# DeltaNet stage with a fixed TensorE order, block-wise operands one job ahead, weight splits on VectorE and DeltaNet's branch as the last jobs

## The chip, the cores and the metric

The kernel runs on one core of one Trainium2 chip. The metric is device time in microseconds: before the change the median of 3 runs is 1790.77 us (1789.58 to 1791.43).

## The reference, cut to what matters

One layer: a modulated norm, three token mixers fed by one input projection, gates, one output projection, then a gated feed-forward part. The sequence has 512 tokens of width 1024 and a context of 256 tokens that only feeds states. All matrices are float32.

```
proj = h @ w_in
s5   = s5_readout(scan(proj[s5]))            # ends in y * sigmoid(y @ s5_w_glu)
dn   = rms(deltanet(q, k, v, beta, g)) * silu(z)   # 8 heads of 128, both directions
cv   = silu(layernorm(dwconv31(a * sigmoid(gate))))
merged = g0 * (s5 @ w_br_s5) + g1 * (dn @ w_br_dn) + g2 * (cv @ w_br_cv)
x = x + mod * (merged @ w_out)
x = x + mod * convffn(rms(x))
```

DeltaNet works in chunks: each head needs, for each chunk and direction, a triangular inverse and a chain over chunks in which a 128x128 state is carried from one to the next.

## The kernel before, in words

A float32 product of full accuracy is made of three float32r matmuls: each operand is split into a high part (ScalarE rounds it) and a low part (the rest, by VectorE or GpSimd). `weights` (L188) loads 128 output columns of a matrix for all 8 blocks of 128 inputs (512 KB, three buffers), and `split` (L178) makes `whi` and `wlo` from it (two buffers each). Which engine makes `wlo` goes by the letters of `split_plan`; in the DeltaNet stage it is "G", so GpSimd makes them.

The stages are: prologue; S5 with the input projections; the convolution's taps; the DeltaNet stage; the output projection (`mix_out`); the feed-forward part. In the S5 stage TensorE's order is kept as written (`tc.manual_schedule`); in the DeltaNet stage the tile scheduler orders all engines by a simulated timeline. Each engine and SyncE, which issues nearly all loads and stores, works its instructions off in the order it is given.

The DeltaNet stage mixes two kinds of work. `dn` (L1516) runs turns. Every 9 turns a new head starts (`dn_head`, L1302), and in a turn each head that is live does one step, up to its next `yield`. A step is a few TensorE operations (float32, 128 columns, two records each) and what VectorE, ScalarE and GpSimd make of them. A head has 47 steps: decays and k-k products; a 15-step elimination on GpSimd (`dn_tmp`, `dn_dd`); doubling of the inverse for s = 16 and 32; a last doubling; 6 chunks of 3 steps each, where `dn_R`, `dn_vt`, `dn_vn`, `dn_S` are made on VectorE and ScalarE; and `dn_out`. So about 5 heads are live at a time. Between the heads' steps `dn` draws from `fill` until the turn has its planned time (3.8 us, in the kernel's own cost units), and from `side` (S5's gelu, the convolution's norm, then the sums for the second modulation, `ada2_sums`) at 2.8 units a turn.

`fill` is `jobs` (L759): 56 jobs, each 128 output columns of a product with 512 tokens, that is 8 steps of 3 matmuls into one PSUM bank. They are 8 for z, 24 for the gates (both on the normed input `hx`), 8 for S5's GLU, 8 for S5's branch and 8 for the convolution's branch. The last three groups have operands of their own: `once` allots a whole operand (`operand`, [128, 8, 512], high and low) and `split_pieces` loads and splits its 8 blocks; at least two blocks are made before the group's first matmul. A job's weights are loaded while the job before it runs; its result is finished (`fin`) after the first step of the next.

When `dn` and the jobs are over, `dn_load` (L1579) loads and splits the eight heads' results, `merged` is loaded as the sum of the two stored branches, and `branch` (L842) makes the 8 jobs of DeltaNet's branch, with the second modulation's sums (`ada2`, one matmul pair with a matrix of ones each) between them.

PSUM: jobs use banks a and e in turn, the heads' preparation and inverse share the two banks of c, the chunk steps use d and b.

Of the kernel before, what the change touches and what calls it, by code (L numbers as in the profile page):

```python
# [8 lines left out]
F32 = mybir.dt.float32  # L9
F32R = mybir.dt.float32r  # L10
# [6 lines left out]
P = 128  # L17
# [33 lines left out]
class Slab:  # L51
# [5 lines left out]
    def tile(self, shape, dtype, **kw):  # L57
# [7 lines left out]
        return t.rearrange("p (a b) -> p a b", a=shape[1]) if len(shape) == 3 else t  # L65

# [13 lines left out]
class Kern:  # L80
# [307 lines left out]
    def modulate_tokens(self, pool):  # L388
# [3 lines left out]
        self.hx = (hp.tile([P, KT, SEQ], F32R, name="hxh"), hp.tile([P, KT, SEQ], F32R, name="hxl"))  # L392
# [366 lines left out]
    def jobs(self, jobs):  # L759

        T = self.nc.tensor
        load = lambda j: self.weights(self.A[j[0]][0], 0, KT, j[1], P)
        jobs = iter(jobs)
        j, done = next(jobs), None
        nxt = load(j)
        while j:
            _, _, xs, fin = j
            (wh, wl), (ps, j) = nxt, (None, next(jobs, None))  # L770
            prep = iter(())
# [9 lines left out]
            ps = self.psum()  # L781
            for k in range(KT):
# [14 lines left out]
    def z_jobs(self, pool):  # L797
# [3 lines left out]
        def fin(h):  # L801
            def f(pz):
                z = pool.tile([P, SEQ], F32, name="do_z", tag="gt", bufs=3)
# [7 lines left out]
    def gate_jobs(self, pool):  # L811
# [3 lines left out]
        def fin(i):  # L815
            def f(pg):
                t = pool.tile([P, SEQ], F32, name="gt", tag="gt", bufs=3)
# [6 lines left out]
    def branch_jobs(self, gi, wname, xs, pool, out, perm=False):  # L824
# [3 lines left out]
        def fin(m):  # L828
            def f(pb):
                sg = pool.tile([P, SEQ], F32, name="br_sg", tag="gt", bufs=3)  # L830
# [11 lines left out]
    def branch(self, gi, wname, xs, pool, tag, bufs, perm=False):  # L842

        nc = self.nc
        for m in range(KT):
            sg = pool.tile([P, SEQ], F32, name="br_sg", tag=tag, bufs=bufs)
            nc.sync.dma_start(sg, self.gt_d[gi * KT + m])
            pb = self.psum()
            self.mm3(pb, self.weights(self.A[wname][0], 0, KT, m * P, P), xs)
            sv, pv = sg, pb  # L850
            if perm:
                sv = sg.rearrange("p (n t) -> p n t", t=8)
                pv = pb.rearrange("p (t n) -> p n t", t=8)
            nc.vector.scalar_tensor_tensor(sv, sv, 1.0, pv, op0=OP.add, op1=OP.mult)
            yield m, sg


    def operand(self, pool, bufs=2):
# [1018 lines left out]
```

## Time and profile before

| | |
|---|---|
| median of 3 runs | 1790.77 us |
| the profiled execution's own time | 1797.43 us |
| its span, first to last instruction | 1795.6 us |
| mean granted TensorE clock | 0.954 |
| TensorE matmuls busy | 1634.2 us |
| VectorE, ScalarE, GpSimd busy | 1143.3, 706.8, 815.2 us |
| data moved | 268.71 MB |

In the profile PE is TensorE's matmuls, PEld its weight loads, DVE VectorE, ACT ScalarE, POOL GpSimd, SP SyncE. Matmul records overlap: one runs on while the next has started, so their sum is longer than the time they need.

### The profile page before, as it was taken

How to read it: one execution, taken by the hardware profiler on the slowest of the kernel's cores; microseconds unless marked ns; L12 is line 12 of the kernel's file. 1: busy time of each engine (PE TensorE's matmuls, PEld its weight loads, DVE VectorE, ACT ScalarE, POOL GpSimd, SP SyncE). 2: the span in 40 equal slices, each digit the busy share in tenths (PEclk: the TensorE clock that was granted, in tenths of full speed). 3: DMA queues.
4: the chain of work that ended last, by engine and by line, in shares of the span. 5: the costliest groups of instructions: out<-in, count | busy, mean ns of one | idle time of the engine just before them, and what ended most of it. 6: DMA issues, size and time to landing. Idle time of an engine off the chain costs nothing.

```text
span 1795.6 us, 25808 instructions
## 1 busy us (share of the span) xinstructions
PE 1634.2 (91%) x9435; PEld 1324.1 (74%) x9435; DVE 1143.3 (64%) x1958; ACT 706.8 (39%) x1422; POOL 815.2 (45%) x978
## 2 busy tenths in 40 slices
PE   7888898989989988988899989998688899999997
PEld 2677787878878436767788878887466688888886
DVE  6775876678788153466664575544355699999324
ACT  4555344434454224333345544433213233443222
POOL 0647867787784336775365554232133011111020
PEclk9899998999999999998999999999899899999999
DMA  8334323343335887878864544745774133333332
GB/s 299 83 84 120 108 73 97 104 115 105 93 92 157 205 231 222 255 222 261 259 197 141 175 138 132 221 146 176 279 241 142 59 94 99 100 94 100 97 95 73
DMA packets 328689, 268.71 MB, mean 150 GB/s; under 512 B 63333, under 2 KB 264818, under 8 KB 328562
## 3 DMA queue, kind: packets, MB, share of 16 engines
q1 hardware_dynamic: 328130, 266.52, 50.0%
q8 instruction: 74, 1.21, 0.3%
q10 hardware_dynamic: 432, 0.54, 0.1%
q14 instruction: 53, 0.43, 0.1%
HBM read 208.62 MB, written 58.39 MB: 149 GB/s over the span
## 4 chain that ended last, share of the span: by engine, by line
PE 58%; DVE 17%; DMA 12%; issue 5%; ACT 5%; POOL 3%; SPq 1%; DVEq 0%; ACTq 0%; POOLq 0%
PE ps_mm L206 9%; PE ps_mm L207 9%; PE ps_mm L208 8%; PE ps_pr L1318 4%; DMA adw<-in_ada_w_dram 3%; PE ps_mm L783 3%; PE ps_mm L788 3%; PE ps_mm L787 3%; PE ps_acc L1600 3%; PE ps_acc L1601 3%; PE ps_acc L1599 3%; PE ps_inv L1318 2%; DVE wlo L185 2%; DVE ad_acc L321 2%; DVE s5G L664 2%
## 5 line engine op out<-in xcount | busy, mean ns | idle before, releaser
L181 ACT ACTIVATE whi<-wraw 128x1024 fp32r<-128x1024 f32 (+1 forms) x187 | 196.6, 1054 | 379.1 <-PE ps_mm L207 195.6
L185 DVE TENSOR_TENSOR wlo<-wraw,whi 128x1024 fp32r<-128x1024 f32 (+1 forms) x131 | 179.7, 1374 | 173.6 <-ACT whi L181 173.0
L185 POOL TENSOR_TENSOR wlo<-wraw,whi 128x1024 fp32r<-128x1024 f32 x56 | 134.7, 2407 | 166.5 <-ACT whi L181 160.0
L206 PE MATMUL ps_mm<-hxh,whi 128*128 128x512 f32 (+1 forms) x392 | 162.6, 415 | 1.9 <-ACT hxh L403 1.9
L207 PE MATMUL ps_mm<-hxl,whi 128*128 128x512 f32 (+1 forms) x392 | 158.3, 404 | 0.7 <-POOL hxl L404 0.7
L208 PE MATMUL ps_mm<-hxh,wlo 128*128 128x512 f32 (+1 forms) x392 | 157.4, 402 | 0.5 <-DVE wlo L185 0.5
L1698 DVE SCALAR_TENSOR_TENSOR f_acc<-fpad,vec,f_acc 128x512 f32<-128x512 f32 x176 | 152.5, 867 | 3.2
L185 POOL TENSOR_TENSOR hidl<-f_acc,hidh 128x512 fp32r<-128x512 f32 x22 | 36.8, 1672 | 243.0 <-ACT hidh L181 243.0
L206 PE MATMUL ps_mm<-h2h,whi 128*128 128x512 f32 x352 | 137.9, 393 | 0.7 <-ACT h2h L1663 0.7
L207 PE MATMUL ps_mm<-h2l,whi 128*128 128x512 f32 x352 | 137.7, 392 | 0.0
L208 PE MATMUL ps_mm<-h2h,wlo 128*128 128x512 f32 x352 | 137.5, 391 | 0.0
L788 PE MATMUL ps_mm<-hxh,wlo 128*128 128x512 f32 x256 | 105.7, 413 | 8.6 <-POOL wlo L185 8.6
L783 PE MATMUL ps_mm<-hxh,whi 128*128 128x512 f32 x256 | 107.1, 418 | 0.0
L787 PE MATMUL ps_mm<-hxl,whi 128*128 128x512 f32 x256 | 105.3, 411 | 0.0
L206 PEld LDWEIGHTS ps_mm<-hxh,whi 128*128 128x128 f32 (+1 forms) x392 | 76.8, 196 | 17.7 <-ACT hxh L403 2.1
L208 PEld LDWEIGHTS ps_mm<-hxh,wlo 128*128 128x128 f32 (+1 forms) x392 | 75.9, 194 | 18.1 <-DVE wlo L185 0.9
L207 PEld LDWEIGHTS ps_mm<-hxl,whi 128*128 128x128 f32 (+1 forms) x392 | 76.2, 194 | 16.4 <-POOL hxl L404 1.2
L783 PE MATMUL ps_mm<-xh,whi 128*128 128x512 f32 x192 | 78.0, 415 | 5.3 <-DVE rs_t L114 5.3
L787 PE MATMUL ps_mm<-xl,whi 128*128 128x512 f32 x192 | 78.7, 410 | 1.5 <-DVE xl L185 1.5
L788 PE MATMUL ps_mm<-xh,wlo 128*128 128x512 f32 x192 | 78.0, 408 | 0.0
L206 PEld LDWEIGHTS ps_mm<-h2h,whi 128*128 128x128 f32 x352 | 66.6, 190 | 14.8 <-ACT h2h L1663 1.1
L207 PEld LDWEIGHTS ps_mm<-h2l,whi 128*128 128x128 f32 x352 | 66.6, 189 | 13.9
(504 smaller groups left out, 4330.7 us busy)
## 6 DMA issues: line engine op xcount, KB each, us to landing
wraw<-in_w_in_dram SPq DMA_DIRECT2D x80, 512.0 KB
wraw<-in_ffn_w_up_dram SPq DMA_DIRECT2D x44, 512.0 KB
adw<-in_ada_w_dram SPq DMA_DIRECT2D x32, 512.0 KB
wraw<-in_ffn_w_down_dram SPq DMA_DIRECT2D x22, 512.0 KB
cv_y<-cvi SPq DMA_DIRECT2D x32, 270.0 KB
adaw<-in_ada_w_dram SPq DMA_DIRECT2D x16, 512.0 KB
h_d<-dn_Hw SPq DMA_DIRECT2D x16, 384.0 KB
dn_Hb<-h_d SPq DMA_DIRECT2D x8, 768.0 KB
```

What stands on the lines that cost most here:

```text
L181: nc.scalar.activation(hi, x, AF.Copy, scale=scale)
L185: (nc.vector if lo_eng == "V" else nc.gpsimd).tensor_tensor(lo, x, hi, op=OP.subtract)
L206: T.matmul(ps, wh[:, k], xh[:, k], start=first and k == 0, stop=False)
L207: T.matmul(ps, wh[:, k], xl[:, k], start=False, stop=False)
L208: T.matmul(ps, wl[:, k], xh[:, k], start=False, stop=last and k == n - 1)
L783: i = T.matmul(ps, wh[:, k], xh[:, k], start=k == 0, stop=False)
L787: T.matmul(ps, wh[:, k], xl[:, k], start=False, stop=False)
L788: T.matmul(ps, wl[:, k], xh[:, k], start=False, stop=k == KT - 1)
L1318: self.dn_mm = T_.matmul(*a, **kw)
L1599: nc.tensor.matmul(ps[i], xh, wh[:, e], start=k == 0, stop=False)
L1600: nc.tensor.matmul(ps[i], xl, wh[:, e], start=False, stop=False)
L1698: V.scalar_tensor_tensor(acc, pad[:, i:i + R, j:j + W], w(t), acc, op0=OP.mult, op1=OP.add)
```

## The change

1. Operands become lists of 8 tiles of [128, 512] (`Parts`, `block`), one tag and one buffer a block, all in the pool that holds `hx`. `made` builds blocks one at a time; `jobs` has blocks 0 to 6 of the next group's operand made during steps 1 to 7 of the last job before it and the eighth in the group's first job. `ready` holds a block back until its input is there.
2. The group order is z, gates, GLU, convolution's branch, S5's branch, DeltaNet's branch. The last is now 8 more jobs (`merge_jobs`), whose blocks are made as heads end; `dn_load` and `branch` are gone. What `dn` does not draw runs after it.
3. TensorE's order in the stage is the written one (`tc.manual_schedule`), during `dn` and after it.
4. `split_plan` stays "V": `wlo` is made on VectorE.
5. A step that yields a negative number gets so much of `fill` at once and goes on: 0.7 ahead of the k-k products (twice), 1.3 between the halves of the transposes of the inverse. The chunk steps issue all their TensorE operations ahead of what reads them, both directions together; q @ S moves to the chunk's first step.
6. A turn is planned at 3.5 instead of 3.8; small tiles (`gt`) have 5 buffers instead of 3, `dn_at` 6 instead of 4; `conv_norm` yields 9 and 6 more units at its end instead of 2.

The diff, cut to its core:

```diff
+class Parts(list):
+    def __getitem__(self, at):
+        return list.__getitem__(self, at[1])[(at[0], *at[2:])]
...
     def jobs(self, jobs):
-            if callable(xs):
-                if done:
-                    done()
-                    done = None
-                prep, xs = xs()
-                for _ in range(2):
-                    yield next(prep)
-            if xs:
-                xh, xl = xs
+            own = None
+            if callable(xs):
+                own, xs = pend
+            if xs:
+                self.cur = xh, xl = xs
+            (wh, wl), j = nxt, next(jobs, None)
+            ahead = None
+            if j and callable(j[2]):
+                pend = j[2]()
+                ahead, new = pend[0], pend[1][0]
             ps = self.psum()
             for k in range(KT):
+                if len(xh) <= k and done:
+                    done()
+                    done = None
+                while len(xh) <= k:
+                    yield next(own)
                 i = T.matmul(ps, wh[:, k], xh[:, k], start=k == 0, stop=False)
...
-                yield max(0.65, next(prep, 0))
+                c = 0
+                if ahead and k and len(new) < KT - 1:
+                    c = next(ahead)
+                elif own:
+                    c = next(own, 0)
+                yield max(0.65, c)
...
+    def merge_jobs(self, gi, wname, xs, pool, then):
+        def fin(m):
+            def f(pb):
+                sg = pool.tile([P, SEQ], F32, name="br_sg", tag="gt", bufs=5)
+                nc.sync.dma_start(sg, self.gt_d[gi * KT + m])
+                t = pool.tile([P, SEQ], F32, name="mg_t", tag="mg_t", bufs=2)
+                a = self.merged[:, m]
+                nc.sync.dma_start(a, self.m_d[0][m])
+                nc.sync.dma_start(t, self.m_d[1][m])
+                nc.gpsimd.tensor_tensor(a, a, t, op=OP.add)
+                nc.vector.scalar_tensor_tensor(sg, sg, 1.0, pb, op0=OP.add, op1=OP.mult)
+                nc.gpsimd.tensor_tensor(a, a, sg, op=OP.add)
+                next(then, None)
+            return f
...
+    def operand(self, pool, n=KT):
+        x = (Parts(), Parts())
+        for _ in range(n):
+            self.block(x, pool)
+        return x
+    def block(self, x, pool):
+        for t, c in zip(x, "hl"):
+            t.append(pool.tile([P, SEQ], F32R, name="x" + c, tag=f"x{c}{len(t)}", bufs=1))
...
+    def made(self, src, pool, scale=1.0, ready=lambda k: True):
+        def f():
+            x = self.operand(None, 0)
+            def pieces():
+                for k in range(KT):
+                    while not ready(k):
+                        yield 0.1
+                    self.block(x, self.hp)
+                    t = pool.tile([P, SEQ], F32, name="ld", tag="gt", bufs=5)
+                    nc.sync.dma_start(t, src[k])
+                    self.split(x[0][:, k], x[1][:, k], t, scale=scale)
+                    yield 0.7
+            return pieces(), x
+        return f
...
     def dn(self, pool, period, turn_time, fill, side, side_rate):
+                while c is not None and c < 0:
+                    more = -c
+                    while more > 0:
+                        c = next(fill, None)
+                        if c is None:
+                            break
+                        more -= c
+                        t += c
+                    c = next(x[0])
...
-                k.split_plan = "G"
...
+                    yield from k.glu_jobs(cur, k.made(k.y2_d, cur))
+                    yield from k.branch_jobs(2, "w_br_cv", k.made(k.cvc, cur, ready=side_done), cur, k.m_d[1])
+                    yield from k.branch_jobs(0, "w_br_s5", k.made(k.s_d, cur, 0.25), cur, k.m_d[0], perm=True)
+                    yield from k.merge_jobs(1, "w_br_dn", k.made([k.dn_d[i * P:(i + 1) * P] for i in range(HEADS)], cur,
+                                                                 ready=lambda i: i < k.heads_done), cur, others())
                 main = k.jobs(work())
-                k.dn(pool, 9, 3.8, main, itertools.chain(side, sums), 2.8)
+                with tc.manual_schedule(engines={nc.tensor.engine}):
+                    k.dn(pool, 9, 3.5, main, itertools.chain(side, sums), 2.8)
                 k.anchors = []
-                for _ in itertools.chain(main, sums):
+                for _ in sums:
                     pass
-            k.h_stack.close()
-            k.psum_plan(mm="abccddde")
             k.split_plan = "V"
...
-                xs = k.dn_load(pool)
...
+                rest = k.ada2(pool)
+                k.psum_plan(mm="abccddde")
+                with tc.manual_schedule(engines={nc.tensor.engine}):
+                    for _ in main:
+                        pass
+            k.h_stack.close()
```

## Rows read from the trace of the kernel before

**Rows 1.** The page, part 1: busy time of TensorE's matmuls, share of the span, instructions.

```profile
PE 1634.2 (91%) x9435; PEld 1324.1 (74%) x9435; DVE 1143.3 (64%) x1958; ACT 706.8 (39%) x1422; POOL 815.2 (45%) x978
```

**Rows 2.** Stretches: length, busy (instructions) of PE, PEld, DVE, ACT, POOL; clock, DMA share, GB/s.

```profile
120.00:560.00 440.00, 401.20 (x2920) 353.28 (x2919) 335.17 (x460) 201.84 (x433) 344.18 (x423) 0.95 0.36 101
676.00:790.00 114.00, 100.93 (x453) 81.22 (x452) 51.52 (x65) 42.99 (x74) 84.73 (x95) 0.97 0.77 231
790.00:916.00 126.00, 110.72 (x662) 93.39 (x662) 83.47 (x123) 46.23 (x104) 69.39 (x98) 0.93 0.85 257
916.00:1044.00 128.00, 120.27 (x807) 106.83 (x807) 68.30 (x164) 65.83 (x172) 71.41 (x111) 0.93 0.56 162
1044.00:1152.00 108.00, 102.33 (x689) 90.06 (x688) 70.92 (x141) 52.15 (x134) 49.75 (x81) 0.97 0.53 154
1152.00:1278.00 126.00, 114.67 (x642) 96.96 (x639) 53.97 (x143) 42.95 (x102) 38.27 (x19) 0.97 0.55 168
1278.00:1354.00 76.00, 58.87 (x212) 42.11 (x212) 34.10 (x38) 13.31 (x16) 22.54 (x16) 0.87 0.81 277
```

**Rows 3.** TensorE's groups by shape, 676 to 1354 us: busy, mean ns, idle before.

```profile
L788 PE MATMUL ps_mm<-hxh,wlo 128*128 128x512 f32 x247 | 102.1, 414 | 8.6 <-POOL wlo L185 8.6
...
L783 PE MATMUL ps_mm<-xh,whi 128*128 128x512 f32 x192 | 78.0, 415 | 5.3 <-DVE rs_t L114 5.3
L1318 PE MATMUL ps_pr<-dn_S,dn_Ha 128*128 128x128 f32 x288 | 54.9, 283 | 4.3 <-DVE dn_o L1509 4.1 <-DVE dn_S L1497 0.2
...
L206 PE MATMUL ps_mm<-xh,whi 128*128 128x512 f32 x64 | 28.0, 448 | 13.6 <-ACT xh L181 13.2 <-ACT whi L181 0.4
...
L1318 PE MATMUL ps_inv<-dn_TT,dn_xm 64*64 64x64 f32 x192 | 14.9, 227 | 3.6 <-ACT dn_xm L1447 3.6
...
L337 PE MATMUL ps_mm<-ad_acc,ones 128*128 128x512 f32 x16 | 8.5, 614 | 2.0 <-DMA ad_acc<-a_d 2.0
...
L1574 PE MATMUL ps_prep<-ident,dn_o 128*128 128x128 f32 x32 | 5.5, 293 | 5.3 <-POOL dn_o L1567 5.3
```

**Rows 4.** TensorE's timeline: start, length of the merged records, their count.

```profile
1002.59 0.39 PE L787 MATMUL ps_mm<-hxl,whi 128*128 128x512 f32 x1
1002.82 0.39 PE L788 MATMUL ps_mm<-hxh,wlo 128*128 128x512 f32 x1
...
1008.81 0.83 PE L1318 MATMUL ps_pr<-dn_R,dn_TT 128*128 128x128 f32 x6
1009.48 0.83 PE L1318 MATMUL ps_inv<-dn_T,dn_nt 128*128 128x128 f32 x6
...
1290.68 0.63 PE L208 MATMUL ps_mm<-xh,wlo 128*128 128x512 f32 x1
1291.11 0.63 PE L206 MATMUL ps_mm<-xh,whi 128*128 128x512 f32 x1
```

**Rows 5.** TensorE's longest waits, 676 to 1354 us: total, times, longest.

```profile
PE ps_mm L206 <- ACT xh L181: 13.2, 3, 9.4
PE ps_prep L1318 <- DVE dn_T L1417: 12.8, 4, 4.3
PE ps_mm L788 <- POOL wlo L185: 8.6, 6, 2.6
PE ps_mm L783 <- DVE rs_t L114: 5.3, 1, 5.3
PE ps_prep L1574 <- POOL dn_o L1567: 5.3, 1, 5.3
```

**Rows 6.** Groups of weight splits: GpSimd in 676 to 1354, VectorE in 120 to 560 us.

```profile
L185 POOL TENSOR_TENSOR wlo<-wraw,whi 128x1024 fp32r<-128x1024 f32 x54 | 129.9, 2407 | 153.3 <-ACT whi L181 146.9 <-ACT dn_S L1499 6.1 <-PE ps_inv L1318 0.3
...
L185 DVE TENSOR_TENSOR wlo<-wraw,whi 128x1024 fp32r<-128x1024 f32 x39 | 58.8, 1507 | 48.6 <-ACT whi L181 48.5
```

**Rows 7.** Durations of single lines' instructions: count, min/median/max in ns, first to last start.

```profile
L1362 DVE TENSOR_TENSOR kkc<-dn_dm,kkc x8: 412/1336/8157, 686.6 to 1058.5; 128x256 f32<-128x256 f32 x8
...
L1383 POOL TENSOR_TENSOR dn_dd<-dn_dd,dn_tmp x120: 209/315/861, 711.0 to 1119.1; 112x15 f32<-112x15 f32 x16, 112x28 f32<-112x28 f32 x16, 112x39 f32<-112x39 f32 x16, 112x48 f32<-112x48 f32 x16
```

More of the change, by code (lines that the diff above doesn't have):

```diff
@@ L765, in jobs @@
         jobs = iter(jobs)
-        j, done = next(jobs), None
+        j, done, pend = next(jobs), None, None
         nxt = load(j)
@@ L1481, in dn_head @@
                     nc.scalar.activation(vt[d], pr[d][:, P:2 * P], AF.Copy, scale=sc(self.et, d))
-            cost = 0.44
-            for d in range(2):
-                c, x = cs[d], xs[d]
-                if x >= 0:
-                    vn[d] = pool.tile([P, P], F32, name="dn_vn", tag="dn_vn", bufs=4)
-                    nc.scalar.activation(vn[d], pr[d][:, P:2 * P], AF.Copy, scale=self.beta[:, c, 8 * d + h:8 * d + h + 1])
-                    mm(pr[d][:, 3 * P:], kq[:, x, 1], S[d], start=True, stop=True)
-                    cost += 0.22
-            yield cost
-            cost = 0.0
+            for d in seq:
+                x = xs[d]
+                vn[d] = pool.tile([P, P], F32, name="dn_vn", tag="dn_vn", bufs=4)
+                nc.scalar.activation(vn[d], pr[d][:, P:2 * P], AF.Copy,
+                                     scale=self.beta[:, cs[d], 8 * d + h:8 * d + h + 1])
+                if x in seen:
+                    V.scalar_tensor_tensor(o[:, x], pr[d][:, 3 * P:], sc(self.eg, d), o[:, x], op0=OP.mult, op1=OP.add)
+                else:
+                    nc.scalar.activation(o[:, x], pr[d][:, 3 * P:], AF.Copy, scale=sc(self.eg, d))
+                seen.add(x)
+            yield 0.44
             if more:
-                for d in range(2):
+                for d in both:
                     mm(pr[d][:, 2 * P:3 * P], ktok[:, cs[d]], vt[d], start=True, stop=True)
+            for d in seq:
+                mm(pr[d][:, :P], At[d][:, xs[d]], vn[d], start=True, stop=True)
+            if more:
+                for d in both:
                     Sn[d] = pool.tile([P, P], F32, name="dn_S", tag="dn_S", bufs=7)
@@ L1499, in dn_head @@
                         nc.scalar.activation(Sn[d], pr[d][:, 2 * P:3 * P], AF.Copy)
-                    cost += 0.22
-            for d in range(2):
-                x = xs[d]
-                if x >= 0:
-                    mm(pr[d][:, :P], At[d][:, x], vn[d], start=True, stop=True)
-                    if x in seen:
-                        V.scalar_tensor_tensor(o[:, x], pr[d][:, 3 * P:], sc(self.eg, d), o[:, x], op0=OP.mult, op1=OP.add)
-                    else:
-                        nc.scalar.activation(o[:, x], pr[d][:, 3 * P:], AF.Copy, scale=sc(self.eg, d))
-                    late.append((lambda a, b: lambda: V.tensor_tensor(a, a, b, op=OP.add))(o[:, x], pr[d][:, :P]))
-                    seen.add(x)
-                    cost += 0.22
+            for d in seq:
+                late.append((lambda a, b: lambda: V.tensor_tensor(a, a, b, op=OP.add))(o[:, xs[d]], pr[d][:, :P]))
+            cost = 0.22 * ((2 if more else 0) + len(seq))
             S = Sn
@@ L1576, in dn_out @@
         nc.sync.dma_start(self.dn_d[h * P:(h + 1) * P], ot)
+        self.heads_done = h + 1
         yield 0.5
-    def dn_load(self, pool):
-        nc = self.nc
-        dh, dl = self.operand(pool, 1)
-        for h in range(HEADS):
-            t = pool.tile([P, SEQ], F32, name="dn_l", tag="dn_l", bufs=3)
-            nc.sync.dma_start(t, self.dn_d[h * P:(h + 1) * P])
-            self.split(dh[:, h], dl[:, h], t)
-        return dh, dl
     def tok_mm(self, xs, nk, w, fin, pool, tail):
@@ L1801, in open_act, with others, side_done @@
+                def others():
+                    yield from rest
+                def side_done(k_):
                     for _ in side:
                         pass
[L1803 removed]
+                    return True
                 def work():
[L1806 to L1810 removed]
@@ L1823, in body @@
             with k.rpool("xs") as pool:
-                xs = k.dn_load(pool)
-                for m in range(KT):
-                    nc.sync.dma_start(k.merged[:, m], k.m_d[0][m])
-                    t = pool.tile([P, SEQ], F32, name="mg_t", tag="mg_t", bufs=2)
-                    nc.sync.dma_start(t, k.m_d[1][m])
-                    nc.gpsimd.tensor_tensor(k.merged[:, m], k.merged[:, m], t, op=OP.add)
-                ada2 = k.ada2(pool)
-                for m, t in k.branch(1, "w_br_dn", xs, pool, "br_sg", 3):
-                    nc.gpsimd.tensor_tensor(k.merged[:, m], k.merged[:, m], t, op=OP.add)
-                    next(ada2)
+                cur.pool = pool
+                rest = k.ada2(pool)
[4 more added lines that the diff above has]
+            k.h_stack.close()
         with ExitStack() as cc:
```

106 lines of the change are left out of this document (44 added, 62 removed).

## The prediction

> **What bounds the kernel now.** The page comes first: TensorE is busy for 91% of the span [rows 1]. That figure is no rate, because a matmul's record overlaps the next one's. So I read the stage between the convolution and the output projection, 676 to 1354 us, in stretches, then its matmuls by shape, then their distance from start to start. In the stretches [rows 2] the reader is to see that TensorE has idle time in each of them (13, 15, 8, 6, 11 and 17 us: 70 us in 678) and that the granted clock stands under 1 everywhere, at 0.87 in the last. Weighted by length it is 0.944. The clock has two levels, 2.4 and 1.2 GHz, so some 11% of the stage ran at the lower one, which costs about 38 us.
>
> How much work is there? [Rows 3] give the counts, [rows 4] the distances: a 512-column matmul starts 0.23 us after the one before it at the full clock, a 128-column one 0.11 us, and behind the wait for DeltaNet's operand [rows 5] the 512-column ones start 0.43 us apart. The 512-column records are 245, 247 and 247 on hx, three times 192 on the later operands and three times 64 in DeltaNet's branch: 1507 x 0.227 = 342 us. Ten groups with 128 columns, the largest of 288 and the smallest of 32 records, make 1408 x 0.111 = 156. The 64-column ones (384, estimated at half of 0.111) make 21, the gate sums (16 x 0.43) 7, and 128 records of other small shapes, estimated at 0.15, 19. That is 545 us of work in 678. Of the 133 us left, 70 are idle and 38 the clock; 25 are small waits and changes between the two kinds of matmul. So TensorE bounds the stage with a fifth of it lost, and whatever this change can gain lies in those 133 us. Transfers are the next bound: the busiest stretches move 257 and 277 GB/s at a DMA share of 0.85 and 0.81 [rows 2], so 300 to 340 GB/s is all there is.
>
> **The change part by part.**
>
> *Operands by block, made one job ahead, and DeltaNet's branch as the last eight jobs.* Before, each group of eight jobs starts by loading and splitting its operand. The waits this leaves on TensorE are the five of [rows 5] without the second and third: 13.2 us for the split of DeltaNet's operand, 5.3 for the last transposes of the last head, behind which nothing stood, 5.3 at the start of the convolution's branch, ended by VectorE, which had a chain of small operations in front of the split. Together 23.8 us. Afterwards the next block is loaded, as soon as the matmul that read its predecessor is over, while the last job of the group before runs, and behind the last head stand whole jobs. I take all 23.8 as gained. If a block comes late, what is late next is the job's k-th matmul. What moves with the branch is 8 loads of `dn_d`, 8 of gates and 16 of the other branches' results, and the 8 gate sums with their 18 loads and 8 stores, all on SyncE behind the jobs' weights; the loads of `x` for the output projection take the operand's place in SBUF and now come after the last job, but are first read when the projection's first sums end. The convolution's norm stands 13 units of side work later, 4.6 turns at 2.8 a turn, and is still over long before its branch.
>
> *The clock* follows the idle time. In the last two stretches, 0.97 over 126 us and 0.87 over 76 us, it costs 3.8 + 9.9 = 13.7 us. With jobs in place of those waits I take 10 back.
>
> *Weights split on VectorE.* GpSimd loses 54 splits of 2.41 us, 130 us [rows 6]. TensorE waited for them 6 times, 8.6 us [rows 5], and I take these as gained. On VectorE a split took 1.51 us in the S5 stage, where GpSimd was busy for 344 of 440 us [rows 2, 6], so the price is at most 54 x 1.51 = 82 us of an engine that had 362 of 678 busy [rows 2]. That lies beside TensorE's work; it costs nothing as long as VectorE's queue is short. Its cover is the turn: each step of a head gives its successor a whole turn of TensorE work. What the row does not bound is blocking: `kkc`, one operation of one shape, took 0.41 to 8.16 us [rows 7], the long ones beside trains of GpSimd operations. The Trainium skill (SBUF — State Buffer, section "Who interferes with whom") says that a VectorE instruction with two SBUF inputs, which this split is, cannot run beside a GpSimd instruction that reads SBUF: one of them blocks altogether. The trace agrees, with those 8.16 us. By this rule the split only changes who blocks, and the sum would be without this step's 8.6 us.
>
> *The kept order.* TensorE now issues a turn's steps as written: 3.5 us of planned work a turn, heads and jobs alternating, and nothing overtakes. There are 7 x 9 + 48 = 111 turns. Before, the scheduler chose the order. The trace cannot price this. From below: the waits inside the heads go (12.8 us on `dn_T` [rows 5], 4.3 and 3.6 in two groups of [rows 3]), and the 25 us of small waits with them, 46 in all. From above: each turn adds one wait of 0.8 us, twice the shortest operation of [rows 7], 111 x 0.8 = 89 us. The new yields with a minus put 0.7 or 1.3 us of jobs just ahead of the steps that share two PSUM banks, among them the one that waited 12.8 us, and I take three quarters of that, 9.6 us, and else nothing: in the stage's steadiest stretch, 1044 to 1152 us, steps and jobs already lie mixed and 5.7 us idle in 108 [rows 2]. Turns of 3.5 in place of 3.8 move jobs behind the last head; no work goes with them.
>
> *Transfers at the end.* The last stretch moved 277 GB/s x 76 us = 21 MB, at a share of 0.81 [rows 2]. With its work of about 51 us (192 x 0.227 + 7) it would want 410 GB/s. At 342, the row's rate at a share of one, it lasts 62. So I charge 12 us (nothing if its loads go out during the jobs before, 25 if it keeps its 76 us). The adds into `merged` change place, not number. The other moved loads and stores (`gt` in five buffers, operand blocks) are the same count on the same SyncE queue.
>
> *Sum:* -23.8 - 10 - 8.6 - 9.6 + 12 = -40 us. The profiled execution took 1797.4 us, 0.4% over the median of 1790.8; -40 on the median is 1750.8, and I say **1750**.
>
> **The rivals.**
>
> *Slower: splits stuck behind GpSimd.* Each head has a train of 15 pairs of GpSimd operations. The second of a pair takes 0.32 us [rows 7], the first by estimate as much: 9.5 us back to back and 76 for eight heads. A split that meets a train can wait as `kkc` did, up to 8.16 us; VectorE's queue, with `dn_R` and `dn_S` of five heads in it, waits behind it, and TensorE, in its kept order, behind those. Some 40 splits fall in the heads' time, which I estimate at 500 us; 76/500 of them, 6, meet a train, and 16 if each of the 206 us that GpSimd keeps counts. At 6 us each, two thirds of it seen by TensorE, that is 24 to 64 us against the gain of 40: from 10 hits on the change is slower. With 14 it takes 1791 - 40 + 56, about 1805. For it: the `kkc` row. Against it: the S5 stage's mean of 1.51, and 130 us less of GpSimd beside all other VectorE work.
>
> *Deeper: idle time and clock go together.* If jobs fill nearly every hole, 70 idle and 38 of clock go, less 12 for the transfers: -96, that is 1695. For it: from 1044 to 1152 us only 5.7 of 108 us are idle [rows 2]. Against it: the heads' chains remain.
>
> *Little: transfers bound it.* From 676 to 916 us the DMA share is already 0.77 and 0.85, and a shorter stage asks for the same bytes in less time. If the loads of weights and heads come later by the 5% that the turns shrink, half the gain of 40 goes, and if the last stretch keeps its 76 us, 13 more are charged: -7, so 1784.
>
> *The change does not do what it says:* the scheduler still orders loads and splits, and may put a block's load where it stood. Then the operand's waits and the clock stay, and the 8.6 us gained at the splits are met by as much on VectorE: 1790, within what a measurement of this kernel can tell from no change, 0.2% or 3.6 us.
>
> **How the numbers follow.** Forecast (1725 to 1775): 0.46. Deeper (below 1725): 0.20. Transfers (1775 to 1787): 0.11. No effect: 0.06. Slower: 0.17. So faster is 0.46 + 0.20 + 0.11 = 0.77, the same 0.06, slower 0.17. The range must leave out no more than 0.2: down to the deeper case, 1692, where 0.04 lie below, and up to 1805, the slower rival's middle, where 0.08 lie above. The forecast alone spans 1725 to 1775 by the bounds of the transfers (0 to 25), the clock (0 to 13.7) and the heads' waits.
>
> **What would show it.** Right: the wait of TensorE on the split of DeltaNet's operand is gone and the last head is followed by 512-column matmuls at 0.23 us; the clock is over 0.95 in every stretch; no `wlo` is on GpSimd, and on VectorE it takes 1.2 to 1.6 us; DMA share in the last jobs is over 0.8. Wrong: `wlo` over 2 us on VectorE with TensorE waiting for `dn_R`, `dn_S` or `dn_xm` (the slower rival), waits on `wraw` or `xh` (transfers), or waits of TensorE that exceed 70 us in the stage. A time over 1787 means that the kept order costs more than it saves.

## The result and the profile after

The changed kernel takes 1759.9 us (median of 4 runs, 1759.5 to 1761.1) against 1790.7 before: a ratio of 0.9826, 95% interval 0.9803 to 0.9848, that is 31 us less. The prediction of 1750 has the right sign and is 10 us too low; its terms are taken up one by one below. The profiled execution took 1761.1 us, its span 1759.3; before, the span was 1795.6. The profiled execution before was 6.7 us longer than its kernel's median, the one after 1.2 us, so what follows compares two spans that differ by 36 us where the medians differ by 31.

First the page, part 1, of the kernel after. GpSimd has lost 118 us against [rows 1], VectorE has gained 17.

```profile
PE 1612.8 (92%) x9435; PEld 1307.0 (74%) x9435; DVE 1160.5 (66%) x2014; ACT 702.0 (40%) x1422; POOL 697.6 (40%) x922
```

Next the stretches of the stage after (columns as in [rows 2]): the stage as a whole, its seven parts (the last head is stored at 1224 us), and two rows that split the stage there. Beneath stands the same split of the kernel before, whose last head is stored at 1281 us.

```profile
676.00:1316.00 640.00, 594.40 (x3499) 500.70 (x3489) 375.34 (x726) 264.01 (x611) 224.49 (x363) 0.98 0.69 212
...
676.00:790.00 114.00, 102.17 (x481) 82.84 (x472) 61.83 (x83) 44.94 (x80) 63.66 (x96) 0.97 0.77 233
790.00:920.00 130.00, 113.79 (x752) 97.12 (x752) 94.24 (x163) 56.27 (x137) 56.89 (x93) 0.97 0.86 264
920.00:1050.00 130.00, 125.38 (x895) 111.48 (x894) 73.64 (x174) 68.73 (x182) 62.01 (x121) 1.00 0.57 169
1050.00:1150.00 100.00, 97.47 (x688) 86.11 (x687) 61.07 (x163) 46.76 (x129) 17.12 (x36) 1.00 0.47 147
1150.00:1224.00 74.00, 70.61 (x358) 59.15 (x358) 40.02 (x99) 24.46 (x58) 2.08 (x2) 0.98 0.58 191
1224.00:1268.00 44.00, 38.98 (x151) 29.90 (x150) 19.50 (x22) 12.25 (x15) 9.99 (x8) 0.89 1.01 335
1268.00:1316.00 48.00, 46.01 (x184) 34.10 (x182) 25.05 (x26) 10.60 (x14) 12.74 (x9) 0.99 0.63 189
...
676.00:1224.00 548.00, 509.42 (x3167) 436.70 (x3158) 330.79 (x679) 241.16 (x582) 201.76 (x347) 0.98 0.66 204
1224.00:1313.00 89.00, 83.57 (x331) 63.51 (x329) 44.08 (x47) 19.85 (x23) 21.44 (x15) 0.94 0.83 264
```

```profile
676.00:1281.00 605.00, 550.02 (x3249) 469.18 (x3247) 328.92 (x636) 250.14 (x584) 314.19 (x401) 0.95 0.65 196
1281.00:1354.00 73.00, 57.75 (x208) 41.40 (x208) 33.35 (x37) 13.31 (x16) 21.89 (x15) 0.88 0.81 271
```

The heads are done 57 us sooner, and the jobs behind them take 16 us more, since more of them stand there. TensorE idles 46 us in the stage where it idled 70. The granted clock, weighted by length over the parts, is 0.978 in place of 0.944: at 1.2 GHz in place of 2.4 the stage now loses 14 us instead of 38. (Idle time at the lower clock counts in both figures, so that they don't add.) From 920 to 1150 us the clock is full. It falls to 0.89 where TensorE idles 5 us in 44 beside a DMA share of 1.01.

TensorE's longest waits in the stage after (engine, what it worked on, what it waited for; total, times, longest):

```profile
PE ps_prep L1361 <- DVE dn_xm L1454: 7.1, 5, 2.3
PE ps_mm L800 <- DVE do_z L828: 5.3, 2, 2.7
PE ps_acc L1650 <- DVE ad_row L350: 5.0, 1, 5.0
PE ps_mm L800 <- ACT xh L193: 4.3, 3, 1.8
PE ps_prep L1361 <- DVE dn_T L1462: 4.1, 3, 2.5
PE ps_inv L1473 <- DVE dn_T L1462: 3.9, 3, 2.4
```

Of [rows 5] the waits on `wlo`, `rs_t` and `dn_o` are gone, `xh` fell from 13.2 to 4.3, and the wait of the heads' preparation (`ps_prep`) on `dn_T` from 12.8 to 4.1 (a second wait on `dn_T`, of the transposes in `ps_inv`, is 3.9 where it was 0.7). New are `do_z`, where a job waits for VectorE to finish an earlier one's result, and `ad_row`: the output projection starts, but its next sum needs a PSUM bank that a gate sum still holds. TensorE's timeline after (start, length, what; in brackets the idle time before and what ended it):

```profile
1312.35 1.13 PE L349 MATMUL ps_mm<-ad_acc,ones 128*128 128x512 f32 x2 [0.40 <-DMA ad_acc<-a_d]
1313.62 0.94 PE L1650 MATMUL ps_acc<-whi,mgh 128*128 128x512 f32 x3
1319.53 0.79 PE L1650 MATMUL ps_acc<-whi,mgh 128*128 128x512 f32 x1 [4.97 <-DVE ad_row L350]
```

And the longest wait of SyncE's queue after, from 1224 to 1316 us (all of it lies behind 1268 us):

```profile
SPq L347 <- DMA g_d<-ad_row: 31.9, 6, 6.0
```

With two buffers, SyncE stands at the load of an `ad_row` until an earlier `ad_row` has been stored, 31.9 us in all, and every load behind it waits too. So 41 us are gained before the output projection's first matmul (1354.7 to 1313.6) and 5 are given back right behind it, which leaves the 36 by which the spans differ.

### The profile page after: what moved, and what is told of

Its sections match the earlier page's. It is cut to its first block, busy times and chain, and to the rows that moved or that the text cites. A ratio compares the mean times of both kernels' runs of the same rounds, so it can differ in the third digit from the quotient of the medians.

```text
span 1759.3 us, 25804 instructions
## 1 busy us (share of the span) xinstructions
PE 1612.8 (92%) x9435; PEld 1307.0 (74%) x9435; DVE 1160.5 (66%) x2014; ACT 702.0 (40%) x1422; POOL 697.6 (40%) x922
## 3 DMA queue, kind: packets, MB, share of 16 engines
q8 instruction: 74, 1.21, 0.3%
## 5 line engine op out<-in xcount | busy, mean ns | idle before, releaser
L800 PE MATMUL ps_mm<-xh,whi 128*128 128x512 f32 x512 | 220.4, 430 | 10.7 <-DVE do_z L828 5.3
L804 PE MATMUL ps_mm<-xl,whi 128*128 128x512 f32 x512 | 203.8, 398 | 3.5 <-DVE xl L197 2.1
L805 PE MATMUL ps_mm<-xh,wlo 128*128 128x512 f32 x512 | 203.3, 397 | 0.0
L218 PE MATMUL ps_mm<-xh,whi 128*128 128x512 f32 (+1 forms) x392 | 162.5, 415 | 1.8 <-ACT xh L415 1.8
L219 PE MATMUL ps_mm<-xl,whi 128*128 128x512 f32 (+1 forms) x392 | 158.1, 403 | 0.7 <-POOL xl L416 0.7
L220 PE MATMUL ps_mm<-xh,wlo 128*128 128x512 f32 (+1 forms) x392 | 157.1, 401 | 0.5 <-DVE wlo L197 0.5
L800 PEld LDWEIGHTS ps_mm<-xh,whi 128*128 128x128 f32 x512 | 98.3, 192 | 32.4 <-DVE do_z L828 6.7
L804 PEld LDWEIGHTS ps_mm<-xl,whi 128*128 128x128 f32 x512 | 98.4, 192 | 22.8 <-DVE xl L197 4.4
L805 PEld LDWEIGHTS ps_mm<-xh,wlo 128*128 128x128 f32 x512 | 97.9, 191 | 21.6
L218 PEld LDWEIGHTS ps_mm<-xh,whi 128*128 128x128 f32 (+1 forms) x392 | 76.6, 195 | 17.7 <-ACT xh L415 2.0
```

Of the source, the lines that this page charges most:

```text
L218: T.matmul(ps, wh[:, k], xh[:, k], start=first and k == 0, stop=False)
L219: T.matmul(ps, wh[:, k], xl[:, k], start=False, stop=False)
L220: T.matmul(ps, wl[:, k], xh[:, k], start=False, stop=last and k == n - 1)
L800: i = T.matmul(ps, wh[:, k], xh[:, k], start=k == 0, stop=False)
L804: T.matmul(ps, wh[:, k], xl[:, k], start=False, stop=False)
L805: T.matmul(ps, wl[:, k], xh[:, k], start=False, stop=k == KT - 1)
```

## The experiments

The ratios are to the kernel before; the changed kernel stands at 0.9826. A difference from it in us is the difference of the ratios times 1790.7, its interval made from the two.

**Parts undone or done alone.**

`undo_vector_splits`: GpSimd makes `wlo` again.

```diff
                 k.dn_lag = 2
+                k.split_plan = "G"
```

> The changed kernel with one part undone: while the heads run, the weights' low parts are made on GpSimd again (the last jobs keep VectorE). Theory of the sum: TensorE's waits on GpSimd's splits come back, 8.6 us and up to 5 of clock, so 1760 + 9 to 14 = 1769 to 1774. First rival (splits on VectorE stuck behind GpSimd's operations cost more than they save): faster, 1740 to 1755, and the waits on do_z (5.3 us) vanish. If neither matters within the heads' slack: 1757 to 1763.

Measured: 1779.3 us, 0.9919 (0.9891 to 0.9948): 17 us (10 to 23) given back, twice the term and above the 9 to 14 expected. The waits on `wlo` are only 5.0 us. Two waits of TensorE in its stage:

```profile
PE ps_inv L1361 <- DMA dn_T<-blk_d: 10.6, 1, 10.6
...
PE ps_mm L805 <- POOL wlo L197: 5.0, 4, 1.7
```

Its GpSimd groups of the splits and of the heads' decays (busy, mean ns, idle before), and beneath them the decays' group of the changed kernel:

```profile
L197 POOL TENSOR_TENSOR wlo<-wraw,whi 128x1024 fp32r<-128x1024 f32 x51 | 121.8, 2388 | 129.2 <-ACT whi L193 127.0 <-PE ps_inv L1361 2.0
L1367 POOL TENSOR_TENSOR dn_ru<-U,Gh 128x384 fp32r<-128x384 f32 x30 | 32.0, 1087 | 20.2 <-PE ps_prep L1361 20.2
```

```profile
L1367 POOL TENSOR_TENSOR dn_ru<-U,Gh 128x384 fp32r<-128x384 f32 x30 | 32.7, 1110 | 76.4 <-PE ps_prep L1361 76.4
```

Without the splits GpSimd idles 76 us ahead of `dn_ru`: it is there when a head asks. With them it idles 20, and TensorE waits 10.6 us for the first head's elimination, whose result goes through memory (`blk_d`). Its operations begin at about 704 us in both kernels. These are its last ones, with GpSimd's splits (seven of them stand between its operations) and in the changed kernel:

```profile
758.58 0.54 POOL L1428 TENSOR_TENSOR dn_dd<-dn_dd,dn_tmp 112x15 f32<-112x15 f32 x1
```

```profile
725.87 0.22 POOL L1428 TENSOR_TENSOR dn_dd<-dn_dd,dn_tmp 112x15 f32<-112x15 f32 x1
```

The stores of the heads' results then begin and end some 16 us later than in the changed kernel (922.1 to 1223.9 us, its row stands below):

```profile
L1635 SPq DMA_DIRECT2D dn_d<-do_t x8: 319/330/1513, 938.7 to 1239.4; - x8
```

So most of the 17 us arises before the first head ends, with GpSimd's queue as the delay that these rows name, and the heads carry it to the end. That it makes up the whole rest is argued, since VectorE's own operations change too. `y`, one of them (row of the changed kernel first, then with GpSimd's splits; least, median, longest in ns):

```profile
L934 DVE SCALAR_TENSOR_TENSOR y<-t,y x8: 683/684/730, 1059.2 to 1145.7; 128x512 f32<-128x512 f32 x8
```

```profile
L934 DVE SCALAR_TENSOR_TENSOR y<-t,y x8: 693/2392/2759, 1070.9 to 1160.3; 128x512 f32<-128x512 f32 x8
```

Seven of the eight start while a split runs on GpSimd and end 0.55 us after it; the eighth, which meets none, takes 0.69 us.

`vector_splits_alone`: the kernel before without its "G".

```diff
-                k.split_plan = "G"
```

> The kernel before with one part of the change alone: the weights' low parts in the DeltaNet stage are made on VectorE. Theory of the sum: 8.6 us of TensorE's waits go, up to 4 of clock: 1791 - 9 to 13 = 1778 to 1782. First rival (VectorE blocked by GpSimd, and its queue in front of the heads' steps): 1795 to 1815. No effect: 1788 to 1794.

Measured: 1780.9 us, 0.9934 (0.9911 to 0.9957), 12 us (8 to 16) faster, inside the expectation for the 8.6 us with their clock. The other waits of [rows 5] are still there, among TensorE's in its stage:

```profile
PE ps_prep L1318 <- DVE dn_T L1417: 14.0, 4, 5.3
PE ps_mm L206 <- ACT xh L181: 11.4, 3, 7.9
PE ps_prep L1574 <- POOL dn_o L1567: 6.6, 1, 6.6
```

Its group of splits on VectorE, 1.37 us each:

```profile
L185 DVE TENSOR_TENSOR wlo<-wraw,whi 128x1024 fp32r<-128x1024 f32 x66 | 90.1, 1366 | 46.7 <-ACT whi L181 46.1 <-DMA br_sg<-gt_d 0.2
```

`undo_kept_order`: the scheduler orders TensorE again (the same edit at the loop over `main` behind `dn`).

```diff
-                with tc.manual_schedule(engines={nc.tensor.engine}):
+                if True:
                     k.dn(pool, 9, 3.5, main, itertools.chain(side, sums), 2.8)
```

> The changed kernel with one part undone: the scheduler orders TensorE in the DeltaNet stage again, all else as changed. Theory of the sum: only the 9.6 us of the heads' waits come back, 1766 to 1772. Rival A, the kept order carries most of the gain (it keeps the heads at 4.9 us a turn in place of 5.4): 1780 or more. Rival B, the kept order costs, since nothing overtakes a late step: below 1755.

Measured: 1774.7 us, 0.9888 (0.9849 to 0.9927): 11 us (3 to 19) given back, between the 1772 at which the theory ended and the 1780 at which rival A began. The heads' ends, first and last, are the starts of the stores in this row; in the changed kernel they are in the second fence.

```profile
L1635 SPq DMA_DIRECT2D dn_d<-do_t x8: 319/343/382, 973.5 to 1259.7; - x8
```

```profile
L1635 SPq DMA_DIRECT2D dn_d<-do_t x8: 319/332/346, 922.1 to 1223.9; - x8
```

The first head ends 51 us later and the last 36: left to itself the scheduler lets jobs go ahead of heads. By 922 us it has issued 660 matmuls of jobs and 470 others, the kept order 564 and 680. The kept order alone in the kernel before was not run.

`undo_lookahead`: no block is made one job ahead.

```diff
-                ahead, new = pend[0], pend[1][0]
+                ahead = None
```

> The changed kernel with one part undone: a group's operand blocks are made in the group's own jobs, the block for a step one step ahead, none during the job before. Theory of the sum: the operand waits come back but for the last head's transposes, 23.8 - 5.3 = 18.5 us and some 5 of clock: 1778 to 1784. Rival, each of the four groups waits at every block because nothing may overtake it in the kept order: 4 x 8 waits of 1 to 2 us, 1792 to 1824. Rival, the loads go out early anyway: 1758 to 1765.

Measured: 1768.9 us, 0.9851 (0.9813 to 0.9890): 4.5 us given back, with an interval from -4 to 13, where I expected about 20; it lies between the theory's range and that of the last rival. Among TensorE's waits in its stage those for split operands did come back, but in small pieces:

```profile
PE ps_mm L800 <- ACT xh L193: 7.6, 7, 1.7
...
PE ps_mm L804 <- DVE xl L197: 3.5, 8, 1.4
```

`dn_branch_before_s5`: DeltaNet's branch is the last but one group; `merge_jobs` now does S5's branch, in its permuted order.

```diff
-                    yield from k.branch_jobs(0, "w_br_s5", k.made(k.s_d, cur, 0.25), cur, k.m_d[0], perm=True)
-                    yield from k.merge_jobs(1, "w_br_dn", k.made([k.dn_d[i * P:(i + 1) * P] for i in range(HEADS)], cur,
-                                                                 ready=lambda i: i < k.heads_done), cur, others())
+                    yield from k.branch_jobs(1, "w_br_dn", k.made([k.dn_d[i * P:(i + 1) * P] for i in range(HEADS)], cur,
+                                                                  ready=lambda i: i < k.heads_done), cur, k.m_d[0])
+                    yield from k.merge_jobs(0, "w_br_s5", k.made(k.s_d, cur, 0.25), cur, others())
```

> The changed kernel with DeltaNet's branch as the last but one group of jobs and S5's branch as the last; the number of jobs, loads and stores is the same. Undoing the look-ahead gave back only 4.5 us of the 23.8 that the sum had for the operands' waits. Theory A (the waits went because whole jobs stand behind the last head, not because blocks are made one job ahead): here the eighth block of DeltaNet's operand is due before the last head is stored, so TensorE again has nothing to put behind the last head's steps and transposes; a wait of 5 to 10 us on that operand or on the heads comes back, the jobs that can't be drawn stand later, and the time is 1768 to 1785. Theory B (the term was too large altogether, since scheduling by block alone hides it): within 5 us of the changed kernel, 1755 to 1765.

Measured: 1764.2 us, 0.9854 (0.9814 to 0.9894): 5 us given back (-3 to 13). The time lies in B's range and not in A's, but the interval reaches A's too, so alone this doesn't decide. The wait that A names is there, among TensorE's in the stage (the profiled execution took 1772.5 us, the longest of its four, so its rows show the most of it):

```profile
PE ps_mm L800 <- ACT xh L193: 10.1, 4, 6.2
```

And its stretch ahead of 1224 us idles 12 us in place of 3, at a clock of 0.92:

```profile
1150.00:1224.00 74.00, 61.60 (x307) 51.16 (x308) 36.08 (x94) 22.41 (x56) 2.08 (x2) 0.92 0.52 170
```

`no_lookahead_dn_before_s5`: the last two edits together.

> The changed kernel with both undone that were undone one at a time before: no block is made one job ahead, and DeltaNet's branch stands before S5's. Alone the first gave back 4.5 us (1768.9) and the second 4.4 (1764.2), against 23.8 in the sum. Theory A (each covers for the other: one job ahead or eight jobs behind, either hides the operand's load and split): together they give back what the sum had, 18 to 30 us, that is 1778 to 1790, and TensorE's wait on the split operand is back at 10 us or more. Theory B (the term was too large by itself; tiles by block already let a group start with its first block): together they give back the sum of the two, 9 us, that is 1765 to 1773.

Measured: 1777.0 us, 0.9935 (0.9913 to 0.9958): 19.5 us (14 to 25) given back. That is in A's 18 to 30, and B's 9 lies outside the interval, so the term itself is confirmed. In the profiled execution (1770.7 us, the shortest of its six runs, so its rows show the least of it) the wait on the operand is over 10 us again:

```profile
PE ps_mm L800 <- ACT xh L193: 15.2, 7, 6.3
```

That each edit hides what the other leaves open is the likelier reading, but not shown: the 10 us by which both together exceed the two alone have an interval from -1 to 21. And the waits on `xh`, 4.3 in the changed kernel, 7.6 and 10.1 with one edit and 15.2 with both, add up nearly as if each edit brought its own.

`before_short_turns`: the kernel before with turns of 3.2.

```diff
-                k.dn(pool, 9, 3.8, main, itertools.chain(side, sums), 2.8)
+                k.dn(pool, 9, 3.2, main, itertools.chain(side, sums), 2.8)
```

> The kernel before with turns planned at 3.2 in place of 3.8, so that whole jobs are left when the last head ends, which DeltaNet's branch waits for. Theory (the operand waits of the sum come from having no job behind the last head, not from late block loads): 13.2 + 5.3 us and some 5 of clock go, 1791 - 18 to 24 = 1767 to 1773. Rival, the scheduler moves jobs forward whatever the plan says: 1786 to 1794. Rival, fewer jobs among the heads leave holes there: 1795 or more.

Measured: 1803.6 us, 1.0063 (1.0045 to 1.0082), 11 us slower, as the last rival had it. Its last head is stored at 1223 us, as in the changed kernel, but up to there TensorE idles 53 us where the changed kernel idles 39, and the clock is 0.93 instead of 0.98:

```profile
676.00:1224.00 548.00, 495.05 (x2979) 428.48 (x2979) 305.82 (x615) 235.56 (x568) 292.53 (x391) 0.93 0.63 187
```

Shorter turns alone are worth nothing: the jobs that leave the turns leave holes there. The two waits that the theory names are gone, but the operand of a group of jobs that now stands behind the heads is waited for instead:

```profile
PE ps_mm L783 <- ACT xh L181: 13.7, 3, 11.7
```

**The end of the stage and the stretch from 790 us.**

`gate_sum_buffers`:

```diff
-        tl = lambda nm: pool.tile([P, 512], F32, name=nm, tag=nm, bufs=2)
+        tl = lambda nm: pool.tile([P, 512], F32, name=nm, tag=nm, bufs=4)
```

> The changed kernel, with four buffers in place of two for the rows of the gate sums that run between DeltaNet's jobs. Theory: in the last jobs SyncE stands for 31.9 us at the load of the next row until an earlier row's store has landed, and the jobs' loads behind it come late; with four buffers that wait goes and the last eight jobs, 7.4 us each now, come near 6.3: 1748 to 1754. Rival, the stretch is bound by the bytes it moves or by VectorE: 1757 to 1762.

Measured: 1755.8 us, 0.9801 (0.9773 to 0.9830), between the two ranges. The 4.5 us are about what TensorE waited for `ad_row`, which is gone from its waits, but the interval (-11 to 2) leaves the sign open. SyncE's wait did not go: it fell from 31.9 to 20.8 us. Like the first, it lies behind 1268 us altogether, so this wait isn't what holds the stretch right behind the last head. That stretch, here from 1220 us, since the heads end 4 us sooner in this execution, is no better:

```profile
SPq L347 <- DMA g_d<-ad_row: 20.8, 4, 6.3
```

```profile
1220.00:1264.00 44.00, 38.03 (x145) 28.23 (x144) 17.73 (x20) 11.24 (x14) 9.49 (x7) 0.89 1.05 352
```

`no_merge_loads` leaves out 15 of the 16 loads of stored branches and adds one tile, loaded once, twice in their place.

```diff
...
-                nc.sync.dma_start(a, self.m_d[0][m])
-                nc.sync.dma_start(t, self.m_d[1][m])
-                nc.gpsimd.tensor_tensor(a, a, t, op=OP.add)
+                nc.gpsimd.tensor_tensor(a, t, t, op=OP.add)
```

> The changed kernel, leaving out 15 of the 16 loads of 256 KB with which the last jobs fetch the two other branches (twice one loaded tile is added instead), operations on the engines the same in number. Theory of the sum (transfers at the end, 12 us charged; the stretch behind the last head has a DMA share of 1.01): 1748 to 1753. Rival, the last jobs go by the chain of the gate sums' buffers on SyncE: 1756 to 1762.

Measured: 1753.8 us, 0.9784 (0.9760 to 0.9809): 7.5 us (1.5 to 13.5) less. In the same stretch TensorE idles 1.6 us, at the full clock:

```profile
1224.00:1268.00 44.00, 42.44 (x179) 32.94 (x178) 22.47 (x26) 13.44 (x16) 12.14 (x10) 1.00 0.89 284
```

SyncE's wait for `ad_row` is as long as ever (33.4 us, behind 1268 us). So right behind the last head, where the share was 1.01, the transfers do bound it. `direct_and_buffers` takes some away and leaves no work out: with four buffers for the gate sums, S5's jobs behind the last head leave their result in `merged`.

```diff
-                sg = pool.tile([P, SEQ], F32, name="br_sg", tag="gt", bufs=5)
+                own = gi == 0 and self.merged is not None
+                sg = self.merged[:, m] if own else pool.tile([P, SEQ], F32, name="br_sg", tag="gt", bufs=5)
...
-                nc.sync.dma_start(a, self.m_d[0][m])
+                if m not in self.direct:
+                    nc.sync.dma_start(a, self.m_d[0][m])
```

> A version of the changed kernel: the jobs of S5's branch that end behind the last head leave their result in the merged tile instead of storing it and loading it again (some 5 jobs, so 10 transfers of 256 KB less, 2.6 MB), and the gate sums' small tiles have 4 buffers instead of 2. Theory A (the last jobs are bound by transfers and by SyncE's queue): at 340 GB/s the 2.6 MB are 7.7 us, and with the 4.5 us that the buffers alone gave the time is 1746 to 1753. Theory B (the two remove the same wait): no better than the buffers alone, 1753 to 1758.

Measured: 1750.8 us (1749.3 to 1756.7), 0.9774 (0.9737 to 0.9812): the best of all versions, 9 us (1 to 17) under the changed kernel. A's range fits; B's, the buffers alone, isn't excluded by the interval.

`fewer_sum_loads` leaves out 24 of the 32 loads of the gate sums (VectorE works on old data instead); `sums_at_half_pace` leaves all in and spreads the sums.

```diff
+                if k0 == 0:
-                raw = pool.tile([P, 2, 512], F32, name="adw", tag="adw", bufs=2)
+                    raw = pool.tile([P, 2, 512], F32, name="adw", tag="adw", bufs=2)
...
```

```diff
-                    yield 0.66
+                    yield 1.32
```

> The changed kernel, leaving out 24 of the 32 loads of 512 KB for the sums of the second modulation (each sum reads its first tile four times), VectorE's operations the same. Theory that transfers bound the stage while it moves 264 GB/s at a share of 0.86 (790 to 920 us, 16 us idle): 1740 to 1750. Rival, the idle time there is VectorE's queue, which has 94 of 130 us busy: 1755 to 1762.

> The changed kernel with the second modulation's sums planned at twice their cost, so that they are spread over about twice the time; nothing is left out. From 790 to 920 us TensorE idles 16 us of 130, with VectorE busy for 94, while taking the sums' loads away there changed nothing. Theory A (VectorE's queue is the limit of this stretch): its idle time falls to 8 to 11 us and the time is 1752 to 1757. Theory B (the heads' own chains are): 1757 to 1763, and the idle time stays at 14 or more.

Measured: 1759.8 us, 0.9820 (0.9795 to 0.9845), and 1763.7 us, 0.9850 (0.9807 to 0.9893). The stretch of the first:

```profile
790.00:920.00 130.00, 117.32 (x773) 101.45 (x772) 96.19 (x172) 55.48 (x135) 65.36 (x109) 0.96 0.60 174
```

The DMA share falls from 0.86 to 0.60, the idle time only from 16 to 13, the time not at all: transfers don't bound this stretch. Half the pace for the sums gave nothing either. Its stretch idles 12 us, between the two theories' figures and by the shortest of its four runs (1754.1 us), with VectorE as busy (96 us of 130). So it didn't take the load off VectorE, and what bounds 790 to 920 us stays open.

## Why the prediction was right, and where its sizes were off

**Operands, 23.8 us: right, and with two covers.** Undoing both covers gives back 19.5 us (14 to 25), with the clock that goes with it. The step named one cause for each wait (blocks made one job ahead; whole jobs behind the last head). By the medians either cause alone does for three quarters of it, so that the first looked worth 4.5 us when it was undone by itself; the intervals don't settle how the two share it. Whole jobs behind the last head without blocks, as in the kernel before with short turns, only moved the wait to another group's operand.

**Weight splits, 8.6 us: right by themselves, mis-sized within the change.** Alone they gave 12 us (8 to 16), which is 8.6 with some clock; undone in the changed kernel they cost 17 (10 to 23). The step counted TensorE's waits on `wlo` alone. In the changed kernel the first head's GpSimd work behind splits of 2.4 us also holds up TensorE (10.6 us on `blk_d`, 0.4 in the kernel before). The price on VectorE was estimated well, at most 82 us for 54 splits: in the stage 63 take 90 us, so 54 take 77. TensorE waits for none of them, though the new wait on `do_z`, 5.3 us here and 1.8 with GpSimd's splits, looks like part of the price. What the step overlooked is in VectorE's total, which rose by 13 us only (from 362, the sum of [rows 2], to 375), though 63 splits of 90 us stand in it now and 9 of 17 us before: its other operations took some 60 us less. `y` took 2.39 us in the median with GpSimd's splits and 0.68 without. The splits in the stage after, as a group of VectorE:

```profile
L197 DVE TENSOR_TENSOR wlo<-wraw,whi 128x1024 fp32r<-128x1024 f32 x63 | 90.3, 1433 | 38.3 <-ACT whi L193 35.8 <-PE ps_prep L1361 1.7 <-PE ps_pr L1361 0.4
```

Durations after (least, median, longest, in ns; first to last start), of the splits and of `kkc`:

```profile
L197 DVE TENSOR_TENSOR wlo<-wraw,whi x63: 1209/1226/2359, 685.4 to 1306.5; 128x1024 fp32r<-128x1024 f32 x63
...
L1407 DVE TENSOR_TENSOR kkc<-dn_dm,kkc x8: 411/613/2077, 689.2 to 1028.1; 128x256 f32<-128x256 f32 x8
```

The slower rival, splits stuck behind GpSimd, priced a hit at up to 8.16 us [rows 7]. The longest split took 2.36 us, 1.13 over its median, and the longest `kkc` came down to 2.08. The rival took the 8.16 us for a meeting with a train of the elimination's short operations. The trace of the kernel before shows that `kkc` (first fence) beside longer operations of GpSimd, nearly back to back, the first of them a split (second fence):

```profile
1058.53 8.16 DVE L1362 TENSOR_TENSOR kkc<-dn_dm,kkc 128x256 f32<-128x256 f32 x1 [0.50 <-ACT dn_dm L1333]
```

```profile
1058.10 2.35 POOL L185 TENSOR_TENSOR wlo<-wraw,whi 128x1024 fp32r<-128x1024 f32 x1
...
1060.59 1.62 POOL L1324 TENSOR_TENSOR dn_ru<-U,Gh 128x384 fp32r<-128x384 f32 x2
...
1063.93 2.47 POOL L1421 TENSOR_TENSOR dn_at<-kk,U 128x512 f32<-128x512 f32 x2
```

With fewer and shorter operations on GpSimd there is less to meet, for the new work and the old. By the Trainium skill (SBUF — State Buffer, section "Who interferes with whom") such a split can't run beside a GpSimd operation that reads SBUF. `y` agrees with it, since it ends only behind the split on GpSimd that it meets, and so does the spread of VectorE's splits from 1.21 to 2.36 us, though at least half of them take close to the least time. But the rival drawn from that rule, that only the blocked side changes, falls with the 12 us of the splits alone.

**Kept order, 9.6 us: the size was right (11, from 3 to 19), the place was not.** The step took three quarters of the wait of `ps_prep` on `dn_T`. That wait fell by 8.7 us, but with the order undone it stays at 4.5:

```profile
PE ps_prep L1361 <- DVE dn_T L1462: 4.5, 3, 2.1
```

So it isn't the order that took it away. Besides, the second wait on `dn_T` rose by 3.2 us, and that of `ps_prep` on `dn_xm` from 1.1 to 7.1. Summed up from the same view, all waits of the heads' steps but for the last transposes fell from 33 to 27 us, 5.5 in place of 9.6, so the size is in part luck. The bound from above took 0.8 us for twice the shortest operation of [rows 7], which is 0.21 us; no term rests on it. What the order does is seen in the heads' ends, 36 us sooner than when the scheduler chooses.

**Clock, 10 us: mis-sized.** I took it from the last two stretches alone. It came back in nearly all: the stage's loss fell from 38 to 14 us, from 0.93 [rows 2] to 1.00 in the stretch from about 920 us too, where TensorE had idled only 8 us. That the clock follows the idle time isn't borne out stretch by stretch: before, it was 0.97 with 13 us idle in 114 and 0.93 with 8 in 128 [rows 2]. What set it there stays open. The sign "over 0.95 in every stretch" failed at 1224 us (0.89).

**Transfers at the end, +12 us: right in kind, and near in size (7.5 us, from 1.5 to 13.5).** Without most of the loads the time is 7.5 us less, and 9 with less data and more buffers. But they bind at 1224 to 1268 us, right behind the last head (share 1.01, 335 GB/s), not in the last jobs (share 0.63). Not foreseen was the 5.0 us of `ad_row` behind the stage.

**Why 31 and not 40.** That the total came so near is in part luck: by the profiles idle time fell by 24 us where the sum had 42 less 12 for the transfers, and the clock gave 24 where the sum had 10 (idle time at the lower clock counts in both). The undone parts add to 17 + 11 + 19.5 = 47.5, less some 8 for the transfers 39.5, yet 31 were measured. The difference is within what the intervals leave open, some 16 us either way. Each part was also undone beside the others, so what two parts gain only together is counted twice. Of the missing 10 us the wait on `ad_row` is 5 by the profile, and the rows were read from an execution 6.7 us over the median; the rest is not settled. No run undid parts 5 and 6 of the change in the changed kernel (the yields with a minus, the chunk steps' order, the turn of 3.5, the buffers), so what they give or cost is open.

The deeper rival, 96 us, fell because the stage still idles 46 us, 28 of them before 920 us, where the first head is not yet done, and 14 us of clock remain. The transfers rival was right at 1224 us and wrong at 790 us.

## What to carry to other kernels

A wait that the trace names is the least that an overloaded engine costs: also look at what else stands in that engine's queue, here the heads' work on GpSimd behind 2.4 us splits, and at other engines' operations that take longer beside it, here VectorE's `y`. When two edits may cover the same stall, undo them together before calling either one worthless. Where work is moved behind a long chain, look at the stretch in which its loads then go out, since here the transfers became the next bound there.

## What the runs showed of the hardware that was not expected

The 1.51 us of a split in the S5 stage [rows 6] are a mean. Half of them took 1.27 us or less, in the changed stage 1.23, with a mean of 1.43: the price is the least time of 1.2 us and a few long meetings. Those of S5 (least, median, longest in ns):

```profile
L185 DVE TENSOR_TENSOR wlo<-wraw,whi x39: 1196/1270/2867, 136.6 to 556.0; 128x1024 fp32r<-128x1024 f32 x39
```

A VectorE operation on two tiles in SBUF (`y`, 0.68 us by itself) that meets a split of 2.4 us on GpSimd ends 0.55 us after that split (seven of seven in `undo_vector_splits`), whatever part of it was left. A load that reuses a buffer whose store is still under way holds SyncE for up to 6.0 us, and all loads behind it.
